# Block sums of gate weights made in the weight queue, a second plain pair at the change of x, and other pacing in a two-sequence encoder layer

## The chip, the cores and the metric

The kernel runs on one core of a Trainium2 chip. The metric is the device time of one execution in microseconds (us); less is better. The engines are TensorE (PE, with its weight loads shown as PEld), VectorE (DVE), ScalarE (ACT), GpSimd (POOL) and SyncE (SP), which issues the transfers that matter here.

## The reference

One encoder layer is applied to two sequences, a prompt of 1024 tokens and a sample of 2048 tokens, each with 16 learned meta tokens ahead of it. All arrays are float32.

```python
def _encoder_layer(h, ...):
    xn = _rmsnorm(h, g_pre)
    proj = xn @ w_in + b_in                      # 1024 -> 6672 columns
    na_q, na_k, na_v, na_z, ml_qk, ml_v, ml_z, ml_o, ml_g, mg = jnp.split(proj, SPLIT_IDX, axis=-1)
    ya = _neighbourhood_attention(na_q, na_k, na_v, na_rpb)     # 8 heads of 64
    ya = (ya * jax.nn.silu(na_z)) @ w_a
    yb = (_mlstm_branch(ml_qk, ml_v, ml_g, ml_o, conv_w, head_g) * jax.nn.silu(ml_z)) @ w_b
    ga, gb = jnp.split(jax.nn.sigmoid(mg), 2, axis=-1)          # 2 x 1024 gate columns
    y = (ga * ya + gb * yb) @ w_out
    return h + _rmsnorm(y, g_post)
```

The neighbourhood attention looks at windows of 8 rows by 16 columns in a grid 64 wide, and at the meta tokens. The mLSTM runs in both directions in chunks of 64 tokens.

## The kernel before

**Arithmetic.** Every float32 factor is split into a high and a low half (`xh`, `xl`; `whi`, `wlo`), and each product is three matmuls, high by high, low by high and high by low (`mm3`, L185 to L187).

**Order.** The order of TensorE's instructions is written out by hand; a scheduler places the instructions of the other engines and the transfers, all of which but a few are issued on SP's queue, and that queue is in order. Two generators give the order. `dense()` walks `PLAN`: groups of columns of the input projection for a sequence s and a half t0 of it, then six final blocks of 512 tokens (merge, output projection, norm).

```python
PLAN = ((0, 0, "m"), (0, 0, "n"), (1, 0, "m"), (1, 1024, "m"), (1, 1024, "n"), (1, 0, "n"), (1, 0, "g"), (1, 1024, "g"), (0, 0, "g"), ("f", 0, 0), ...)
```

"m" are the mLSTM's columns, "n" the attention's, "g" the 16 blocks of gate columns; s = 0 is the prompt, s = 1 the sample. `sparse()` gives the steps of the recurrence and of the attention: `ml` of s = 0, `na` of s = 0, `ml` of s = 1, `na` of s = 1. `run()` puts the two together: each step of the sparse generator yields a credit (`A_NA` for the attention, `A_A` and others for the mLSTM), and the dense generator then runs until the costs of its matmuls (`C512` = 0.235 for one of 512 columns) have used the credit up. A greater credit thus puts more dense matmuls beside each step.

**Weights.** A queue (`requests`) lists all weights in the order of their use. `wload` (L249) fetches the raw ones into one of two buffers (`wraw`, L257); `wpump` (L260) splits them on ACT (L286) and DVE (L287) into one of four pairs of buffers (`whi`, `wlo`; `NBW` = 4), and stores the halves for later uses (L307); a weight that was kept comes back by two loads (L279). `wtake` takes the next ones of the queue and `wdone` gives a buffer back and pumps on. The 16 weights of the merge and the output projection (kinds "m" and "o") are split and stored ahead of time, one ahead of each job of the groups 3 to 5 of `PLAN` (7, 5 and 4 of them). A job is four columns in feature-major form, or one token-major unit (`tm_unit`).

**Gates of the sample.** For s = 1 the gate columns are worked out in pairs of column blocks by a Strassen-Winograd scheme with seven products in place of eight (`sgates`): 84 matmuls of 512 columns for a pair, half and group where the plain way has 96. It needs sums of blocks of the weights and of x. The sums of weights are made by `wprep`: for each of the eight pairs two raw loads of 512 KB (`pr`), sums on DVE (`ps`), a split on ACT (`po`, L560) and on DVE (L561), and eight stores (`q..<-po`, L564). `wprep` is a side generator that is advanced at every second turn (`pace`) of the dense generator (`beside`); its first loads go out in the opening, and its transfers reach into (0,0,n). The sums of x are made by `tprep` (L588 to L599, stores at L602), at (1,1024,n) and (1,0,n), also as a side generator. At the gates the sums are loaded back (`whi<-q`, L272; `t1h` and so on, L855).

**The change of x.** Between (1,0,g) and (1,1024,g) the sample's other half must be loaded (`xload`, L863, and the sums of x, L855). `lead(j)` names the pairs that are worked out plainly at the start of such a group, as they need only x itself; there is one, pair 0. Each plain pair is run on the first 512 tokens and then on the second.

**Places that the prediction speaks of.** L1206 loads the mLSTM's gates (`g_t`). L1062 to L1089 are the attention's loads for one head pair (`gt`, `qr`, `kr`, `vr`, `zt`), L637 and L645 the stores of projected columns (`mq`, `nq`, `nz`), L527 the stores of split x for later groups, L1126 to L1173 the attention's scores, transposes and outputs.

Of the kernel before, what the change touches and what calls it, by code (L numbers as in the profile page):

```python
# [9 lines left out]
F32 = mybir.dt.float32  # L10
F32R = mybir.dt.float32r
I32 = mybir.dt.int32
AF = mybir.ActivationFunctionType
ALU = mybir.AluOpType
# [3 lines left out]
P = 128  # L18
TCARGS = dict(schedule_with_timeline_sim=True)
D = 1024  # L20
KT = D // P
# [9 lines left out]
C_MQ, C_MK, C_MV, C_MZ, C_MO, C_GA, C_GB = 2048, 2560, 3072, 3584, 4096, 4624, 5648  # L31
# [9 lines left out]
PLAN = ((0, 0, "m"), (0, 0, "n"), (1, 0, "m"), (1, 1024, "m"), (1, 1024, "n"), (1, 0, "n"), (1, 0, "g"), (1, 1024, "g"), (0, 0, "g"), ("f", 0, 0), ("f", 0, 1), ("f", 1, 0), ("f", 1, 1), ("f", 1, 2), ("f", 1, 3))  # L41
SW = ((1, 0), (1, 1024))
OPS = ("11", "12", "21", "22", "s1", "s2", "s3", "s4")
STEPS = (("ml", 0, ()), ("na", 0, (0, 1)), ("ml", 1, ()), ("na", 1, (0, 1, 2, 3)))
KC0 = (0, 8, 24, 40)
NKB = (3, 4, 4, 3)
# [83 lines left out]

NBW = 4
C512, C256 = 0.235, 0.12
A_NA, A_D, A_A, A_G = 1.085, 1.63, 1.82, 1.3


class K:
# [3 lines left out]
    def __init__(self, tc, ins, outs):  # L140
        self.tc, self.nc = tc, tc.nc
        self.xs = []
        self.i, self.o = ins, outs
        self.wreq, self.wraw, self.wrdy, self.wout = deque(), deque(), deque(), 0
        self.wseen, self.wkept, self.xkept = set(), {}, {}
        self.rwait = {}
        self.xput, self.turn, self.last, self.turns = deque(), 0, None, False
        self.need = False
        self.hold, self.early = deque(), True
        self.side, self.qd, self.TD = None, {}, {}  # L150


    def rsqrt8(self, pool, v, shape):
# [94 lines left out]

    def wload(self, most=2):  # L249

        while self.wreq and sum(x[1] is not None for x in self.wraw) < most:
            key, src, nk, w = self.wreq.popleft()
            raw = None
            if key[0] != "q" and key not in self.wseen:
                self.wseen.add(key)
                raw = self.wrp[0].tile([P, 4 * WU], F32, name="wraw", bufs=self.wrp[1])
                self.nc.sync.dma_start(raw[:, :nk * w], src)  # L257
            self.wraw.append((key, raw, nk, w))

    def wpump(self, most=NBW, parts=1, copy=None):  # L260


        nc, wp = self.nc, self.wp
        self.wload()
        while self.wraw and self.wout < most:
            key, raw, nk, w = self.wraw.popleft()
            n = nk * w
            hi = wp.tile([P, 4 * WU], F32R, name="whi", bufs=NBW)
            lo = wp.tile([P, 4 * WU], F32R, name="wlo", bufs=NBW)
            if key[0] == "q":  # L270
                for x, k in zip((hi, lo), key[1:]):
                    nc.sync.dma_start(x[:, :n].bitcast(F32), self.qd[k][:, :])  # L272
                self.wrdy.append([x[:, :n].rearrange("p (h k c) -> p h k c", h=2, k=4) for x in (hi, lo)])
                self.wout += 1
                self.wload()
                continue
            if raw is None:
                for x, d in zip((hi, lo), self.wkept[key]):
                    nc.sync.dma_start(x[:, :n].bitcast(F32), d[:, :])  # L279
            else:  # L280
                for a in range(parts):
                    c = slice(a * n // parts, (a + 1) * n // parts)
                    if copy:
                        copy(hi[:, c], raw[:, c])
                    else:
                        nc.scalar.activation(hi[:, c], raw[:, c], AF.Copy)  # L286
                    nc.vector.tensor_tensor(lo[:, c], raw[:, c], hi[:, c].bitcast(F32), op=ALU.subtract)  # L287
                self.wkept[key] = []
                for x, part in ((hi, "h"), (lo, "l")):
                    d = self.dp.tile([P, n], F32, name=f"w{part}{len(self.wkept)}")  # L290
                    self.hold.append((d, x[:, :n].bitcast(F32)))
                    self.wkept[key].append(d)
                if not self.early:
                    self.wflush()
                if key[0] in "mo":
                    self.wrdy.append(None)
                    self.wout += 1
                    self.wload()
                    continue
            self.wrdy.append([x[:, :n].rearrange("p (k c) -> p k c", k=nk) for x in (hi, lo)])  # L300
            self.wout += 1
            self.wload()
# [5 lines left out]

    def wtake(self, n):
        self.wpump()  # L310
        while self.wrdy[0] is None:
            self.wrdy.popleft()
            self.wdone()
        return [self.wrdy.popleft() for _ in range(n)]

    def wdone(self, n=1):
        self.wout -= n
# [125 lines left out]
    def build_half(self, s, t0, res):  # L443

        nc, wp = self.nc, self.wp
        if (s, t0) in self.xkept:
            yield
            yield "scaled"
            x = []
# [7 lines left out]
        if s == 0:  # L457
# [22 lines left out]
            def rows():  # L480
                self.rrows(dg, self.rr[:, 1], "sm")
                self.RD = self.dp.tile([P, D], F32, name="rrd")
                nc.sync.dma_start(self.RD[:, :], self.rr.rearrange("p a t -> p (a t)"))
                self.xp.close()
                self.side, self.pace = self.wprep(), 2
            self.rwait[s, t0] = rows
        else:
            bp = self.bp
# [47 lines left out]
    def wprep(self):  # L536
# [3 lines left out]
        with self.tc.tile_pool(name="pq", bufs=1, side="right", reuse_waits="tile") as pool:  # L540
            raws = {}

            def load(p):
                if p < 8:
                    raws[p] = pool.tile([P, 2, 2, 512], F32, name="pr", bufs=2)
                    for f in range(2):
                        nc.sync.dma_start(raws[p][:, f].rearrange("p a c -> p (a c)"), self.i["wu"][unit["i", C_GA + (2 * p + f) * P, P], :, :D])

            load(0)
            load(1)  # L550
            for _ in range(4):
                yield
            for p in range(8):
                raw = raws.pop(p)
                sm = pool.tile([P, 4, 512], F32, name="ps", bufs=1)
                todo = [((p, "11"), (p, "12"), raw[:, 0]), ((p, "21"), (p, "22"), raw[:, 1]),
# [219 lines left out]

    def lead(self, j):

        return [] if PLAN[j - 1][:2] == PLAN[j][:2] else [0]

    def requests(self):

        unit = {k: j for j, k in enumerate(_weight_units())}
        ahead = deque([("m", f, P) for f in range(KT)] + [("o", c, a) for c in range(4) for a in range(2)])
        for j, (s, t0, cols) in enumerate(PLAN):
            if s == "f":
                assert not ahead
                keys = [("m", f, P) for f in range(KT)] + [("o", c, a) for c in range(4) for a in range(2)]
            else:
                keys = []  # L790
                for kind, c in self.layout(cols):
                    if j >= 3 and ahead:
                        keys.append(ahead.popleft())
                    if cols == "g":
                        continue
                    keys += [("i", x, P) for x in c] if kind == "fm" else [("t", *c, a) for a in range(2)]
                if cols == "g":
                    assert not ahead
                    pairs = list(range(8))
                    lead = pairs if (s, t0) not in SW else self.lead(j)  # L800
                    keys = [("q", (p, f + "1"), (p, f + "2")) for p in lead for f in "12"]
                    pairs = [p for p in pairs if p not in lead]
                    if pairs:
                        seq = _sw_order(pairs)
                        keys += [("q", *seq[x:x + 2]) for x in range(0, len(seq), 2)]
            for k in keys:
                if k[0] == "q":
                    self.wreq.append((k, None, KT, P))
                    continue
                nk, w = (KT, P) if k[0] in "im" else (4, k[2] if k[0] == "t" else 256)  # L810
                self.wreq.append((k, self.i["wu"][unit[k], :, :nk * w], nk, w))
# [16 lines left out]

    def gopen(self):

        assert not any(x[1] is not None for x in self.wraw)
        self.left.close()
        self.gp, self.bp = self.left.enter_context(self.tc.tile_pool(name="gp", bufs=1, reuse_waits="tile")), None

# [100 lines left out]
    def group(self, s, t0, meta, cols, reuse, nxt):  # L935
# [3 lines left out]
        nb = None  # L939
        sw = (s, t0) in SW and cols == "n"  # L940
        if sw:
            self.side, self.pace = self.tprep(s, t0), 2
            sw = (s, t0, "g") in PLAN[:PLAN.index((s, t0, "n")) + 2]
        for j, (kind, c) in enumerate(jobs):
            if kind == "tm":
# [49 lines left out]
    def na(self, s, rts):  # L995
# [3 lines left out]
        with tc.tile_pool(name=f"na{s}{rts[0]}", bufs=1, side="right", reuse_waits="tile") as np_:  # L999
# [12 lines left out]
            for k in range(6):  # L1012
                next(prep, None)
                for _ in range(2 if k else 17 - 11 * s):
                    yield A_NA
            cur, nxt = self.head, None
            units = [(j, cb) for j in range(n) for cb in range(4)]
            ready = {}
# [1 line left out]
            for u in range(n_ + 4):  # L1020
                if u >= 4:
                    self.na_copy(ready[u - 4])
                if u < n_:
# [6 lines left out]
                    self.na_scores(np_, ready[u], rows)  # L1030
                    if j + 1 < n and cb == 0:
                        self.na_bias(rows, heads, j + 1)
                yield A_NA
                if u < n_:
                    self.na_exp(np_, ready[u])
                if 1 <= u <= n_:
# [4 lines left out]
                    next(prep, None)  # L1041
                if u == n_ + 3:
                    break
                yield A_NA
                if 2 <= u <= n_ + 1:
                    self.na_turn(np_, ready[u - 2])
                    if u < n_ and cb >= 2:
                        next(prep, None)
                yield A_NA
                if 2 <= u <= n_ + 1:  # L1050
                    self.na_low(ready[u - 2])
                if u >= 3:
                    self.na_out(ready[u - 3])
                yield A_NA

    def na_bias(self, rows, heads, j):

# [1003 lines left out]
```

## Time and profile before

| | before |
|---|---|
| median of 3 runs | 2819.14 us (2814.47 to 2819.79) |
| profiled execution | 2815.92 us |
| its span | 2814.2 us |
| its mean granted TensorE clock | 0.982 |
| HBM | 516.46 MB read, 244.69 MB written |

The stages of the plan start, in the profiled execution and by the order of TensorE's instructions, at 7.7 us (0,0,m), 277.7 (0,0,n), 508.0 (1,0,m), 774.2 (1,1024,m), 1063.3 (1,1024,n), 1278.5 (1,0,n), 1503.7 (1,0,g), 1690.1 (1,1024,g), 1901.9 (0,0,g), and the last final block at 2690.3. `na` of s = 0 begins at 779.8, `ml` of s = 1 at 1181.3 and `na` of s = 1 at 1998.0. Times in the profile are us from the start of the span, means of one instruction are in ns. The bracket behind an instruction of the time line is the idle time of its engine ahead of it, and what ended it.

### The profile page before, as it was taken

Reading aid. Unit: us, or ns where it says so; the run is one execution under the profiler, and the core shown is the slowest. Engines: PE = TensorE matmul, PEld = TensorE weight load, DVE = VectorE, ACT = ScalarE, POOL = GpSimd, SP = SyncE. Lnnn points to the kernel's source line nnn. Section 1 sums busy time; section 2 is a strip of 40 time slices with the busy share of each in tenths; the row PEclk is TensorE's granted clock in tenths of the full one; section 3 lists DMA queues with packets and bytes.
Section 4 is the critical chain, followed back from the end, with each engine's and each line's share of the span. In section 5 each row is a group of like instructions: output and inputs, shape, how many; then the busy total and the mean of one; then the engine's idle time right before and its main releaser. Section 6 shows DMA issues by size and latency. Waiting matters only on the chain.

```text
span 2814.2 us, 47371 instructions
## 1 busy us (share of the span) xinstructions
PE 2703.1 (96%) x16132; PEld 2379.4 (85%) x16132; DVE 1887.8 (67%) x5176; ACT 1394.3 (50%) x3305; POOL 16.3 (1%) x100
## 2 busy tenths in 40 slices
PE   9699799999999999999999997999999999999988
PEld 7599698889878988887798885888888998989978
DVE  4445478866657665467866754757468889798864
ACT  5332355653446455355546553555355655655531
POOL 0000000000000000000000000000000000000000
PEclk9899899999999999999999998999999999999989
DMA  9999666966697756479778889888669798998945
GB/s 364 397 387 365 238 211 229 365 204 199 213 352 267 228 194 214 158 246 341 269 251 283 278 284 351 289 284 296 190 195 303 242 323 271 298 323 265 322 163 212
DMA packets 397970, 764.32 MB, mean 272 GB/s; under 512 B 50240, under 2 KB 179216, under 8 KB 396192
## 3 DMA queue, kind: packets, MB, share of 16 engines
q1 hardware_dynamic: 396608, 758.61, 79.6%
q0 software_dynamic: 1120, 2.69, 0.4%
q8 instruction: 127, 2.08, 0.3%
q14 instruction: 115, 0.94, 0.1%
HBM read 516.46 MB, written 244.69 MB: 270 GB/s over the span
## 4 chain that ended last, share of the span: by engine, by line
PE 84%; DMA 10%; DVE 3%; ACT 1%; SPq 1%; issue 1%; DVEq 0%; POOL 0%; ACTq 0%; POOLq 0%
PE pj L185 12%; PE pj L187 12%; PE pj L186 12%; PE pj L707 5%; PE pj L708 5%; PE pj L709 5%; PE pj L890 3%; PE pj L892 3%; PE pj L891 3%; PE pj L1824 3%; PE pj L1826 3%; PE pj L1825 3%; PE sm L1173 3%; PE tr L1158 2%; DMA xl<-xl 1%; DMA xt<-xt 1%
## 5 line engine op out<-in xcount | busy, mean ns | idle before, releaser
L185 PE MATMUL pj<-xh,whi 128*128 128x512 f32 (+1 forms) x1360 | 535.7, 394 | 46.2 <-ACT st L627 23.1
L186 PE MATMUL pj<-xl,whi 128*128 128x512 f32 (+1 forms) x1360 | 523.0, 385 | 5.5 <-DMA xl<-xl 5.1
L187 PE MATMUL pj<-xh,wlo 128*128 128x512 f32 (+1 forms) x1360 | 521.8, 384 | 3.7 <-DMA wlo<-wl 3.4
L185 PEld LDWEIGHTS pj<-xh,whi 128*128 128x128 f32 x1360 | 258.5, 190 | 92.0 <-ACT st L627 23.5
L707 PE MATMUL pj<-whi,xh 128*128 128x256 f32 (+1 forms) x1152 | 329.0, 286 | 0.6 <-DVE stT L722 0.6
L708 PE MATMUL pj<-wlo,xh 128*128 128x256 f32 (+1 forms) x1152 | 324.9, 282 | 0.0
L709 PE MATMUL pj<-whi,xl 128*128 128x256 f32 (+1 forms) x1152 | 324.7, 282 | 0.0
L187 PEld LDWEIGHTS pj<-xh,wlo 128*128 128x128 f32 x1360 | 258.2, 190 | 58.1 <-DMA wlo<-wl 4.7
L186 PEld LDWEIGHTS pj<-xl,whi 128*128 128x128 f32 x1360 | 258.7, 190 | 47.7 <-DMA xl<-xl 5.6
L1824 PE MATMUL pj<-whi,mh 128*128 128x256 f32 x768 | 220.6, 287 | 0.7 <-DMA whi<-wh 0.7
L707 PEld LDWEIGHTS pj<-whi,xh 128*128 128x128 f32 x1152 | 216.9, 188 | 1.0 <-DVE stT L722 0.8
L708 PEld LDWEIGHTS pj<-wlo,xh 128*128 128x128 f32 x1152 | 217.0, 188 | 0.1
L709 PEld LDWEIGHTS pj<-whi,xl 128*128 128x128 f32 x1152 | 217.0, 188 | 0.0
L1826 PE MATMUL pj<-whi,mlo 128*128 128x256 f32 x768 | 216.3, 282 | 0.0
L1825 PE MATMUL pj<-wlo,mh 128*128 128x256 f32 x768 | 216.0, 281 | 0.0
L185 PE MATMUL pj<-yh,whi 128*128 128x512 f32 x384 | 155.0, 404 | 5.1 <-ACT yh L1742 5.1
L1165 DVE TENSOR_TENSOR pts<-tr,pts 96x384 fp32r<-96x384 f32 (+2 forms) x192 | 118.8, 619 | 57.2 <-ACT pts L1160 55.3
L187 PE MATMUL pj<-yh,wlo 128*128 128x512 f32 x384 | 152.3, 397 | 0.0
L186 PE MATMUL pj<-yl,whi 128*128 128x512 f32 x384 | 152.0, 396 | 0.0
L1160 ACT ACTIVATE pts<-tr 96x384 fp32r<-96x384 f32 (+2 forms) x192 | 103.5, 539 | 89.8 <-PE tr L1158 89.2
L1824 PEld LDWEIGHTS pj<-whi,mh 128*128 128x128 f32 x768 | 145.1, 189 | 1.8 <-DMA whi<-wh 0.9
L1825 PEld LDWEIGHTS pj<-wlo,mh 128*128 128x128 f32 x768 | 145.1, 189 | 0.9
(367 smaller groups left out, 6142.9 us busy)
## 6 DMA issues: line engine op xcount, KB each, us to landing
whi<-wh SPq DMA_DIRECT2D x160, 512.0 KB
wlo<-wl SPq DMA_DIRECT2D x160, 512.0 KB
wraw<-wu SPq DMA_DIRECT2D x48, 512.0 KB
wh<-whi SPq DMA_DIRECT2D x48, 512.0 KB
wl<-wlo SPq DMA_DIRECT2D x48, 512.0 KB
gt<-st SPq DMA_DIRECT2D x96, 256.0 KB
tg<-gt SPq DMA_DIRECT2D x96, 256.0 KB
whi<-q SPq DMA_DIRECT2D x43, 512.0 KB
```

Source lines behind the costliest of these rows:

```text
L185: mm(out, ah, bh, start=start, stop=False)
L186: mm(out, ah, bl, start=False, stop=False)
L187: mm(out, al, bh, start=False, stop=stop)
L707: nc.tensor.matmul(o, xh, wh, start=k == 0, stop=False)
L708: nc.tensor.matmul(o, xh, wl, start=False, stop=False)
L709: nc.tensor.matmul(o, xl, wh, start=False, stop=k == KT - 1)
L890: mm(bank, w[:, 0, k], xh[:, k], start=fresh and k == 0, stop=False, skip_group_check=True)
L1160: nc.scalar.activation(pts[:ks, :nb, 0, :], pt[:ks, :nb], AF.Copy)
L1165: self.nc.vector.tensor_tensor(pts[:ks, :nb, 1, :], pt[:ks, :nb], pts[:ks, :nb, 0, :].bitcast(F32), op=ALU.subtract)
L1824: nc.tensor.matmul(o, mh[:, k, xs], wh, start=clear > 0 and k == 0, stop=False)
L1825: nc.tensor.matmul(o, mh[:, k, xs], wl, start=False, stop=False)
L1826: nc.tensor.matmul(o, ml[:, k, xs], wh, start=False, stop=clear < 2 and k == KT - 1)
```

## The change

There are three parts.

1. **Block sums.** `wprep` makes the sums of the first three pairs only (`EARLY`), at every fourth turn in place of every second, and after six idle turns in place of four. For the other five pairs there are 20 entries ("p", pair, n) in the weight queue, four for each pair. Entries 0 and 1 fetch the two raw blocks, which stay in the two raw buffers (`pk`) until entry 3 is through; entries 2 and 3 make the sums in place on DVE. Each entry is split, in halves of 512 columns, into a `whi` and a `wlo` buffer, and stored by two transfers of 512 KB. `AHEAD` spreads these entries and then the 16 merge and output weights over groups 2 to 5 of the plan: 7, 7, 6 entries of sums in groups 2, 3 and 4, 6 merge weights in group 4 and 10 in group 5. They now stand between the weights of a job, where before the merge weights stood ahead of a job.
2. **Two plain pairs.** `lead` gives pairs 0 and 1 at the change of x.
3. **Pacing.** The attention's credit is 0.94 for s = 0 (1.085 before) and stays 1.085 for s = 1; `A_A` is 1.79 (1.82 before); `tprep` is advanced at every third turn (second before).

The counts of the built kernels: 16120 matmuls on TensorE (16108 before), 3004 activations (2987), 2455 two-tensor operations on DVE (2437), 2400 transfers on SP (2403).

```diff
+EARLY = 3
+AHEAD = ((0, 0), (0, 0), (1, 1), (1, 1), (2, 3), (2, 4))
-A_NA, A_D, A_A, A_G = 1.085, 1.63, 1.82, 1.3
+A_N, A_D, A_A, A_G = (0.94, 1.085), 1.63, 1.79, 1.3
...
     def wload(self, most=2):
-        while self.wreq and sum(x[1] is not None for x in self.wraw) < most:
-            key, src, nk, w = self.wreq.popleft()
+        while self.wreq:
+            key, src, nk, w = self.wreq[0]
             raw = None
-            if key[0] != "q" and key not in self.wseen:
+            if src is not None and key not in self.wseen:
+                if sum(x[1] is not None for x in self.wraw) + len(self.pk) >= most:
+                    break
...
+    def wsums(self, key, raw, x):
+        nc = self.nc
+        _, p, n = key
+        if raw is not None:
+            self.pk.append(raw[:, :D].rearrange("p (a c) -> p a c", a=2))
+        r = self.pk
+        sub = lambda o, a, b: nc.vector.tensor_tensor(o, a, b, op=ALU.subtract)
+        if n == 2:
+            nc.vector.tensor_tensor(r[1][:, 1], r[1][:, 0], r[1][:, 1], op=ALU.add)
+            sub(r[1][:, 0], r[0][:, 0], r[1][:, 0])
+        elif n == 3:
+            sub(r[0][:, 0], r[1][:, 1], r[0][:, 0])
+            sub(r[0][:, 1], r[0][:, 1], r[0][:, 0])
+        v = r[n % 2 if n < 2 else 3 - n]
+        for q, op in enumerate((("11", "12"), ("21", "22"), ("s3", "s1"), ("s2", "s4"))[n]):
+            h = x[q][:, :512]
+            nc.scalar.activation(h, v[:, q], AF.Copy)
+            nc.vector.tensor_tensor(x[q][:, 512:D], v[:, q], h.bitcast(F32), op=ALU.subtract)
+            d = self.qd[p, op] = self.dp.tile([P, D], F32, name=f"q{p}{op}")
+            nc.sync.dma_start(d[:, :], x[q][:, :D].bitcast(F32))
+        if n == 3:
+            self.pk = []
...
     def wpump(self, most=NBW, parts=1, copy=None):
+            if key[0] == "p":
+                self.wsums(key, raw, (hi, lo))
+                self.wrdy.append(None)
+                self.wout += 1
+                self.wload()
+                continue
...
     def wtake(self, n):
         self.wpump()
-        while self.wrdy[0] is None:
-            self.wrdy.popleft()
-            self.wdone()
-        return [self.wrdy.popleft() for _ in range(n)]
+        out = []
+        while len(out) < n:
+            x = self.wrdy.popleft()
+            if x is None:
+                self.wdone()
+            else:
+                out.append(x)
+        return out
...
-                self.side, self.pace = self.wprep(), 2
+                self.side, self.pace = self.wprep(), 4
...
-        return [] if PLAN[j - 1][:2] == PLAN[j][:2] else [0]
+        return [] if PLAN[j - 1][:2] == PLAN[j][:2] else [0, 1]
...
     def requests(self):
-        ahead = deque([("m", f, P) for f in range(KT)] + [("o", c, a) for c in range(4) for a in range(2)])
+        merge = [("m", f, P) for f in range(KT)] + [("o", c, a) for c in range(4) for a in range(2)]
+        ahead = deque([("p", p, n) for p in range(EARLY, 8) for n in range(4)] + merge)
...
-                for kind, c in self.layout(cols):
-                    if j >= 3 and ahead:
-                        keys.append(ahead.popleft())
+                for n, (kind, c) in enumerate(jobs):
+                    mine = [("i", x, P) for x in c] if kind == "fm" else [("t", *c, a) for a in range(2)]
+                    more = AHEAD[j][kind == "tm"] if j < 5 or n + 1 < len(jobs) else 0
+                    for u, k in enumerate(mine):
+                        for _ in range((u + 1) * more // len(mine) - u * more // len(mine)):
+                            if ahead:
+                                keys.append(ahead.popleft())
+                        keys.append(k)
...
-            self.side, self.pace = self.tprep(s, t0), 2
+            self.side, self.pace = self.tprep(s, t0), 3
...
-                yield A_NA
+                yield A_N[s]
```

More of the change, by code (lines that the diff above doesn't have):

```diff
@@ L257, in wload @@
                 self.nc.sync.dma_start(raw[:, :nk * w], src)
+            self.wreq.popleft()
             self.wraw.append((key, raw, nk, w))
+    def wsums(self, key, raw, x):
[19 more added lines that the diff above has]
+        if n == 3:
+            self.pk = []
     def wpump(self, most=NBW, parts=1, copy=None):
@@ L543, in load @@
             def load(p):
-                if p < 8:
+                if p < EARLY:
                     raws[p] = pool.tile([P, 2, 2, 512], F32, name="pr", bufs=2)
@@ L550, in wprep @@
             load(1)
-            for _ in range(4):
+            for _ in range(6):
                 yield
-            for p in range(8):
+            for p in range(EARLY):
                 raw = raws.pop(p)
@@ L787, in requests @@
                 assert not ahead
-                keys = [("m", f, P) for f in range(KT)] + [("o", c, a) for c in range(4) for a in range(2)]
+                keys = merge
+            elif cols == "g":
+                assert not ahead
+                pairs = list(range(8))
+                lead = pairs if (s, t0) not in SW else self.lead(j)
+                keys = [("q", (p, f + "1"), (p, f + "2")) for p in lead for f in "12"]
+                pairs = [p for p in pairs if p not in lead]
+                if pairs:
+                    seq = _sw_order(pairs)
+                    keys += [("q", *seq[x:x + 2]) for x in range(0, len(seq), 2)]
@@ L789, in requests @@
             else:
                 keys = []
-                for kind, c in self.layout(cols):
-                    if j >= 3 and ahead:
-                        keys.append(ahead.popleft())
[L794 to L805, printed above, removed]
+                jobs = self.layout(cols)
@@ L806, in requests @@
             for k in keys:
-                if k[0] == "q":
+                if k[0] == "q" or k[0] == "p" and k[2] > 1:
                     self.wreq.append((k, None, KT, P))
+                    continue
+                if k[0] == "p":
+                    self.wreq.append((k, self.i["wu"][unit["i", C_GA + (2 * k[1] + k[2]) * P, P], :, :D], KT, P))
                     continue
@@ L829, in gopen @@
     def gopen(self):
-        assert not any(x[1] is not None for x in self.wraw)
+        assert not self.pk and not any(x[1] is not None for x in self.wraw)
         self.left.close()
@@ L1032, in na @@
                         self.na_bias(rows, heads, j + 1)
-                yield A_NA
+                yield A_N[s]
                 if u < n_:
@@ L1043, in na @@
                     break
-                yield A_NA
+                yield A_N[s]
                 if 2 <= u <= n_ + 1:
@@ L1048, in na @@
                         next(prep, None)
-                yield A_NA
+                yield A_N[s]
                 if 2 <= u <= n_ + 1:
@@ L1053, in na @@
                     self.na_out(ready[u - 3])
-                yield A_NA
+                yield A_N[s]
     def na_bias(self, rows, heads, j):
```

## The prediction

> **What bounds the kernel now.** I read the page's totals first, then TensorE's waits, then the time line and the chain around each long wait, and last the order in which the instructions of both built kernels stand on each queue.
>
> ```profile
> span 2814.2 us, 47371 instructions
> PE 2703.1 (96%) x16132; PEld 2379.4 (85%) x16132; DVE 1887.8 (67%) x5176; ACT 1394.3 (50%) x3305; POOL 16.3 (1%) x100
> PE pj L185 <- ACT st L627: 23.1, 1, 23.1
> ```
>
> TensorE is busy for 2703.1 of 2814.2 us. The change leaves its work nearly alone, so all that it can win lies in the 111.1 us of idle time (2814.2 - 2703.1), and what it can lose are new holes. The largest hole, 23.1 us (third row: idle total, times, longest), lies in the opening, where both kernels issue the same transfers in the same order; it stays. The other large holes are three, and the change touches each. The run profiled took 2815.92 us, 1.7 us more than its span; the median of the three runs is 2819.14, 3.2 us above it. I make the sum against 2815.92.
>
> **The block sums leave the opening.** In the time line (start, duration, engine, line, tiles; in brackets the idle time before and its releaser), the chain and the windows (PE, PEld, DVE, ACT, POOL busy, PEclk, DMA share, GB/s):
>
> ```profile
> 296.69 3.27 SPq L564 DMA_DIRECT2D q7s<-po  x4
> 304.33 0.42 SPq L1206 DMA_DIRECT2D g_t<-gg  x1
> 298.86 5.02 DMA q7s<-po
> 310.86 1.07 PE L1233 MATMUL sm<-g_lf,tri 128*128 128x36 f32 x4 [16.06 <-DVE g_lf L1227]
> 311.00:317.00 6.00, 6.00 (x23) 4.47 (x23) 1.51 (x6) 0.49 (x3) 0.00 (x0) 0.61 0.00 0
> ```
>
> The last sums of pair 7 are stored at 296.69, land 5.02 us after 298.86, and only then do the gates of the mLSTM (g_t) load, at 304.33; TensorE stands for 16.06 us. It then runs 6 us at a granted clock of 0.61, which loses (1 - 0.61) x 6 = 2.3 us. In the changed order the last store of the three early pairs stands ahead of this place, and g_t's load has moved far ahead of it: -18.3 us (bounds: 0 if the load still meets a wait, -18.3). What is late next here is nothing that the trace shows; the stage behind it has its weights.
>
> The Trainium skill, "TensorE: Matmul & The Clock Gate", Part 1, has the array drop to half speed after an idle window of about 3.4 us and come back after as long a busy one; the 0.61 after the 16.06 us hole agrees. By the page a hole over 3.4 us loses about 1.7 us of clock (an estimate) where I take 2.3, which would make the sum less than 1 us lower.
>
> The work itself goes into later stages:
>
> ```profile
> L560 ACT ACTIVATE po<-pr 128x1024 fp32r<-128x1024 f32 x16 | 16.8, 1050 | 5.8 <-DMA pr<-wu 3.4 <-DMA q<-po 2.0 <-DMA q0s<-po 0.4
> L561 DVE TENSOR_TENSOR po<-pr,po 128x1024 fp32r<-128x1024 f32 x16 | 19.5, 1220 | 8.3 <-ACT po L560 8.3
> 290.00 0.69 ACT L622 ACTIVATE st<-pj,bq 128x512 f32<-128x512 f32 x1 [3.02 <-DVE pj L620]
> ```
>
> Twenty entries of 1.05 us ACT and 1.22 us DVE, now in halves of 512. Two halves take 2 x 0.69 us (third row) where a whole takes 1.05, a third more: 7 us of ACT and at most 8 us of DVE over four stages. ACT (50%) and DVE (67%) hide that except where DVE is full, which I cost below. It costs nothing as work; it costs as order.
>
> **One more pair done plainly at the change of x.**
>
> ```profile
> 1720.11 0.80 PE L185 MATMUL pj<-xh,whi 128*128 128x512 f32 x1 [15.24 <-DMA xh<-xh]
> 1725.98 0.80 PE L186 MATMUL pj<-xl,whi 128*128 128x512 f32 x1 [5.08 <-DMA xl<-xl]
> 1690.00:1705.00 15.00, 14.86 (x79) 12.50 (x77) 9.89 (x35) 8.27 (x23) 0.00 (x0) 1.00 1.03 407
> 1705.00:1726.00 21.00, 0.82 (x2) 0.31 (x2) 4.72 (x23) 1.82 (x5) 0.00 (x0) 0.58 1.04 403
> 530.20 0.40 PE L185 MATMUL pj<-xh,whi 128*128 128x512 f32 x1
> 530.43 0.40 PE L186 MATMUL pj<-xl,whi 128*128 128x512 f32 x1
> ```
>
> The stage starts at 1690. TensorE has work for 15 us (48 plain matmuls on the first half of x, 31 others), then stands 20.3 us (15.24 + 5.08), as the second half of x arrives 36 us after the start. The DMA engines are full over the whole stretch (share 1.03 and 1.04). The changed kernel moves the same x and sums there, so I keep the 36 us. It has 96 plain matmuls at 0.233 us (spacing of the last two rows), 22.4 us, and some 5.2 us of the mLSTM between: 27.6 us of work, so 8.4 us of hole. That wins 11.9 us. A plain pair costs 96 matmuls per stage against 84: 12 x 0.233 = 2.8 us. Together -9.1 us (bounds: +2.8 if x is later by as much, -14.7 if it came in 30 us).
>
> **The pace: neighbourhood attention ends before the last block.**
>
> ```profile
> 2698.83 1.22 PE L1173 MATMUL sm<-pts,vt 104*128 104x256 f32 x4 [3.49 <-ACT prb L1141]
> 2703.10 0.60 PE L1126 MATMUL sm<-kd,stk 128*128 128x312 f32 x1 [1.07 <-ACT prb L1141]
> 2709.50 0.62 PE L1173 MATMUL sm<-pts,vt 104*128 104x256 f32 x3 [0.59 <-DVE pts L1165]
> 2717.29 0.79 PE L185 MATMUL pj<-yh,whi 128*128 128x512 f32 x1 [5.07 <-ACT yh L1742]
> 2690.00:2720.00 30.00, 19.63 (x87) 16.02 (x86) 17.88 (x61) 10.10 (x29) 0.00 (x0) 0.75 0.19 63
> ```
>
> Now it ends 66 instructions into the last final block; its last units and the block's y wait for each other (3.49 + 1.07 + 0.59 + 5.07 = 10.2 us), with the clock at 0.75 over the 30 us. In the changed order it ends 204 matmuls ahead of that block, so other matmuls fill these waits: -10.2, and 1.5 of clock, -11.7 us (bounds 0 and -11.7). The same density costs elsewhere: each unit of s = 0 has some 13% less dense work beside it (0.94 against 1.085). Its chain of scores, exponentials and transposes then shows in places, between 0 and the 5.2 us (3.49 + 1.07 + 0.59) that it shows at the end, where it has none beside it. I take +2. The slower pace of the x sums puts their vector work at the same place in the built order, so nothing.
>
> **The new places in the weight queue.** SP issues in order, so a load behind a store waits for what the store waits for. The Trainium skill, "DMA: Bandwidth & Descriptors", Anatomy of one DMA, says the same: the DMA engines wait on no semaphore, the issuing sequencer does, ahead of dispatch. That speaks against this change; g_t at 304.33, behind the sums' stores, agrees. The changed order puts the load of the fourth column's weights 0 to 12 TensorE instructions ahead of its use at several starts of stages, behind stores of the columns before, since its slot comes free later with sum tiles between. At (1,0,m):
>
> ```profile
> 524.88 0.42 SPq L637 DMA_DIRECT2D mq<-st  x1
> 525.39 3.68 SPq L527 DMA_DIRECT2D xh<-xh  x6
> 529.17 2.19 SPq L527 DMA_DIRECT2D xl<-xl  x2
> 500.00:550.00 50.00, 50.00 (x249) 41.63 (x249) 43.27 (x143) 36.05 (x88) 0.20 (x2) 1.00 1.00 355
> 2782.62 4.61 DMA whi<-wh
> 1689.14 11.75 DMA whi<-q
> ```
>
> The load now stands behind these stores of mq and x, so it goes out at 529.1 to 531.4; the column is wanted at 530.7, when the third one's last matmuls (530.20, 530.43) are through. A weight needs 4.61 to 11.75 us to land (the last two rows, start and duration), with the DMA engines full here (share 1.00) nearer the middle: 8 us of hole and 2.3 of clock, +10.3 (bounds 0 and +14). At (1,1024,m):
>
> ```profile
> 774.40 0.47 PE L185 MATMUL pj<-xh,whi 128*128 128x512 f32 x1 [1.80 <-DMA whi<-wh]
> 785.92 0.50 PE L187 MATMUL pj<-xh,wlo 128*128 128x512 f32 x1 [2.48 <-DMA wlo<-wl]
> 791.35 0.42 SPq L1062 DMA_DIRECT2D gt<-rpb  x1
> 794.59 0.72 SPq L1089 DMA_DIRECT2D zt<-nz  x1
> 798.17 1.47 SPq L527 DMA_DIRECT2D xh<-xh  x2
> 798.66 0.39 PE L186 MATMUL pj<-xl,whi 128*128 128x512 f32 x1
> ```
>
> The late load stands behind the attention's seven loads (791.35 to 795.3) and x's stores (to 799.6), and is wanted at 798.9. By the long landing it is there at 811.4: 12.5 of hole and 2.3 of clock; the two waits of now, 4.3 us, lie in front of it and go: +10.5 (bounds -4.3 and +17). One more such load stands ahead of the first token-major unit of (1,1024,n): +4, by the 4.61 (0 to +12). At (1,0,n):
>
> ```profile
> 1314.73 0.36 PE L1574 MATMUL sc<-q,kh 128*128 128x256 f32 x1 [3.75 <-DVE den L1624]
> 1344.68 0.36 PE L1574 MATMUL sc<-q,kh 128*128 128x256 f32 x1 [2.62 <-DVE den L1621]
> 1362.47 1.01 PE L1705 MATMUL tr<-ident,hb 128*128 128x128 f32 x4 [3.67 <-DVE hb L1700]
> 1300.00:1350.00 50.00, 43.64 (x212) 36.26 (x212) 47.37 (x121) 32.14 (x80) 0.10 (x1) 0.97 0.93 311
> 1304.18 0.32 SPq L602 DMA_DIRECT2D t0h<-xr  x1
> ```
>
> Here DVE is full (47.37 of 50) and TensorE waits for it three times, 10.0 us. The fourth load now stands behind the store of column three and those of the x sums (as at 1304.18), which wait for this full DVE: by the long landing 11.75 and 2.3 of clock, 14 us. Two more weights with no lead cost 4.61 each, 9 us. Six more merge weights are split here (10 against 4), 7.3 us of DVE, of which I let 5 show. That is 28 us in place of the 10.0: +18 (bounds -5 and +30).
>
> **Sum:** -18.3 - 9.1 - 11.7 = -39.1; +2 + 10.3 + 10.5 + 4 + 18 = +44.8; +5.7 us, 2815.92 + 5.7 = 2821.6, so 2822. A measurement of this kernel tells about 0.2% (5.6 us) from no change.
>
> **Rivals.** *The late loads are in time.* If the sequencer stands less long than the order allows, each of six late loads costs what a late weight costs now (2.48) less the 4.3 that go, 10.6; with +2 for attention and the DVE waits as they are, -39.1 + 12.6 = -26.5, so 2789. For it: the trace shows many loads land in 4.61. Against: at 304.33 a queue wait was paid in full. *The queue's waits add up (slower).* If all six late loads land like the 11.75 row behind full DMA engines, each costs some 4.2 us more than I took (mean of mine 7.6): +5.7 + 25 = +31, 2847. It decides once the DMA share of (1,0,m) and (1,1024,m) stays at 1.0 until the late load. For it: shares of 1.00 and 0.93 already. *x comes later.* With the extra weights ahead of it, the second half of x is needed and late alike: the 11.9 go, 2834. *The gates' wait is not removed*, as g_t meets another late store: +18.3, 2840.
>
> **How the numbers follow.** The forecast gets 0.43 (2810 to 2834: 12 either way, the distance from its largest cost, 18, to that one's upper bound), loads in time 0.30, queue adds up 0.15, x later 0.07, gates' wait stays 0.05. Faster by over 0.2%: all of loads in time and 0.04 of the forecast, 0.34. Within 0.2%: 0.18, from the forecast alone. Slower: the rest, 0.21 + 0.15 + 0.07 + 0.05 = 0.48. The range leaves out half of the worst case and a little of the best: 2792 to 2844.
>
> **What would show it.** Right: no hole near 295 to 311; about 8 us behind 96 plain matmuls at the second stage of gates; no wait at the last final block; holes of 8 to 14 us released by whi or wlo at the fourth columns of (1,0,m), (1,1024,m) and (1,0,n). Wrong: those fourth columns start with holes under 3 us (then 2789), or with over 15 us each (then 2847).

## The result and the profile after

| | before | after |
|---|---|---|
| median (10 runs each) | 2816.85 us (2811.64 to 2819.79) | 2825.02 us (2822.89 to 2828.5) |
| ratio, 95% interval | | 1.0031 [1.0021, 1.004] |
| profiled execution | 2815.92 us | 2825.11 us |
| its span, granted clock | 2814.2 us, 0.982 | 2823.4 us, 0.980 |

The change makes the kernel slower by 0.31%, some 8.7 us. The forecast was 2822. The page of the changed kernel begins:

```profile
span 2823.4 us, 47431 instructions
PE 2708.3 (96%) x16144; PEld 2383.2 (84%) x16144; DVE 1886.9 (67%) x5194; ACT 1394.2 (49%) x3322; POOL 16.2 (1%) x100
```

The span grew by 9.2 us. TensorE is busy for 5.2 us more, of which the 12 matmuls of the second plain pair are 2.8 (12 x 0.233); the granted clock is lower too (0.982 to 0.980). Its idle time grew from 111.1 to 115.1 us (2823.4 - 2708.3). This small difference hides a large exchange. TensorE's waits of the changed kernel (idle total, times, longest):

```profile
PE pj L188 <- DMA whi<-wh: 29.9, 4, 12.5
PE pj L188 <- ACT st L667: 23.9, 1, 23.9
PE pj L747 <- DMA whi<-wh: 18.6, 2, 13.3
PE pj L190 <- DMA wlo<-wl: 6.0, 3, 2.8
PE pj L188 <- DMA wlo<-q: 5.9, 2, 3.6
PE pj L748 <- DMA wlo<-wl: 4.9, 2, 3.8
```

But for the opening's 23.9 us, all the waits at the head of the list are now for weights or their sums; before, the longest waits for a loaded weight were 1.80 us (whi) and 2.48 us (wlo). The windows (PE, PEld, DVE, ACT, POOL busy, PEclk, DMA share, GB/s) show what went:

```profile
290.00:311.00 21.00, 20.64 (x99) 15.27 (x98) 7.57 (x39) 7.72 (x19) 0.00 (x0) 1.00 0.16 53
311.00:317.00 6.00, 6.00 (x28) 4.85 (x27) 3.78 (x10) 3.32 (x8) 0.00 (x0) 1.00 0.99 342
1740.00:1770.00 30.00, 23.86 (x95) 19.15 (x94) 10.05 (x39) 8.29 (x21) 0.00 (x0) 0.83 1.03 404
2690.00:2720.00 30.00, 30.00 (x254) 30.00 (x253) 10.17 (x22) 8.95 (x28) 0.00 (x0) 1.00 0.57 195
2720.00:2750.00 30.00, 30.00 (x151) 25.29 (x151) 18.34 (x40) 4.95 (x13) 0.00 (x0) 1.00 0.78 270
```

The gates' hole near 300 us is gone, and the clock behind it is 1.00; at the change of x (now at 1733) 6.1 us of idle are left in the window in place of 20.3; and the last attention units (2690 to 2720) and the start of the last block, which is now at 2724.6 with the attention done at 2697, have no idle time (last two rows). And this is what came, in the time line of TensorE and of SP, with two steps of the chain:

```profile
515.99 0.77 PE L188 MATMUL pj<-xh,whi 128*128 128x512 f32 x1 [4.42 <-DMA whi<-wh]
792.21 0.77 PE L188 MATMUL pj<-xh,whi 128*128 128x512 f32 x1 [12.50 <-DMA whi<-wh]
1186.89 0.58 PE L747 MATMUL pj<-whi,xh 128*128 128x256 f32 x1 [13.30 <-DMA whi<-wh]
1326.63 0.79 PE L188 MATMUL pj<-xh,whi 128*128 128x512 f32 x1 [10.63 <-DMA whi<-wh]
1392.49 0.79 PE L190 MATMUL pj<-xh,wlo 128*128 128x512 f32 x1 [2.77 <-DMA wlo<-wl]
1435.21 0.58 PE L747 MATMUL pj<-whi,xh 128*128 128x256 f32 x1 [5.26 <-DMA whi<-wh]
...
779.36 0.69 SPq L1109 DMA_DIRECT2D gt<-rpb  x1
783.77 0.35 SPq L1136 DMA_DIRECT2D zt<-nz  x1
784.50 0.34 SPq L315 DMA_DIRECT2D whi<-wh  x1
784.50 7.58 DMA whi<-wh
...
1179.40 0.48 SPq L315 DMA_DIRECT2D whi<-wh  x1
1318.55 0.42 SPq L642 DMA_DIRECT2D t1h<-xr  x1
1321.06 0.63 SPq L315 DMA_DIRECT2D whi<-wh  x1
```

At (1,1024,m) the fourth column is wanted at 779.7 (792.21 - 12.50). Its load goes out at 784.50, behind the attention's loads, and takes 7.58 us to land. At 1173.6 (1186.89 - 13.30) and 1316.0 (1326.63 - 10.63) the loads are late too: they go out 5.8 and 5.1 us after they are wanted, the second behind stores of the x sums.

### The profile page after: what moved, and what is told of

The parts are those of the page before. It is cut to its first block, busy times and chain, and to the rows that moved or that the text cites. A ratio compares the mean times of both kernels' runs of the same rounds, so it can differ in the third digit from the quotient of the medians.

```text
span 2823.4 us, 47431 instructions
## 1 busy us (share of the span) xinstructions
PE 2708.3 (96%) x16144; PEld 2383.2 (84%) x16144; DVE 1886.9 (67%) x5194; ACT 1394.2 (49%) x3322; POOL 16.2 (1%) x100
## 2 busy tenths in 40 slices
DMA packets 397540, 762.76 MB, mean 270 GB/s; under 512 B 50193, under 2 KB 179169, under 8 KB 395761
## 3 DMA queue, kind: packets, MB, share of 16 engines
HBM read 514.89 MB, written 244.69 MB: 269 GB/s over the span
## 4 chain that ended last, share of the span: by engine, by line
PE 82%; DMA 10%; DVE 3%; ACT 2%; SPq 1%; issue 1%; DVEq 0%; ACTq 0%
PE pj L188 12%; PE pj L190 12%; PE pj L189 12%; PE pj L747 5%; PE pj L748 5%; PE pj L749 5%; PE pj L1871 3%; PE pj L1872 3%; PE pj L1873 3%; PE pj L937 3%; PE pj L939 3%; PE pj L938 3%; PE sm L1220 3%; PE tr L1205 2%; DMA wlo<-wl 1%
## 5 line engine op out<-in xcount | busy, mean ns | idle before, releaser
L188 PE MATMUL pj<-xh,whi 128*128 128x512 f32 (+1 forms) x1376 | 544.4, 396 | 57.5 <-DMA whi<-wh 29.9
L190 PE MATMUL pj<-xh,wlo 128*128 128x512 f32 (+1 forms) x1376 | 529.9, 385 | 6.3 <-DMA wlo<-wl 6.0
L189 PE MATMUL pj<-xl,whi 128*128 128x512 f32 (+1 forms) x1376 | 530.0, 385 | 0.1
```

The lines of the kernel that those rows point to most:

```text
L188: mm(out, ah, bh, start=start, stop=False)
L189: mm(out, ah, bl, start=False, stop=False)
L190: mm(out, al, bh, start=False, stop=stop)
```

## The experiments

Ratios are to the kernel before, measured beside it on the same chip; their medians before were 2814.0 to 2817.8 us.

| kernel | median, us | ratio, 95% interval |
|---|---|---|
| e1: change, entries ahead of a job | 2793.76 | 0.9927 [0.9915, 0.994] |
| e2: before, two plain pairs | 2796.23 | 0.9938 [0.9926, 0.9951] |
| e3: before, pacing | 2791.8 | 0.9918 [0.9904, 0.9931] |
| e4: before, two plain pairs and pacing | 2779.34 | 0.9871 [0.9856, 0.9886] |
| e5: before, slower sums of x | 2814.41 | 1.0002 [0.9994, 1.0011] |
| e6: before, attention credit of s = 0 | 2791.19 | 0.9916 [0.99, 0.9932] |
| e7: change, six pairs early, entries ahead | 2770.81 | 0.9848 [0.9834, 0.9861] |
| e8: before, block sums in the queue | 2831.51 | 1.0064 [1.0046, 1.0081] |
| e9: change, all entries ahead of jobs | 2809.34 | 0.997 [0.996, 0.9979] |
| e10: e7 with seven pairs early | 2783.28 | 0.9876 [0.986, 0.9891] |

**e1: the same work, other places in the queue.**

```diff
                     for u, k in enumerate(mine):
-                        for _ in range((u + 1) * more // len(mine) - u * more // len(mine)):
+                        for _ in range(0 if u else more):
```

> The changed kernel with one edit: the entries of sums and merge weights stand ahead of the first weight of a job, as the merge weights did in the kernel before, and not between its weights. Same work, same counts. Theory (place in the queue): the late loads are the fourth weights whose buffer is freed by an entry that stands just ahead of them. In the built order the leads of these loads at (1,0,m), (1,1024,m) and (1,0,n) grow from 0 to 12 TensorE instructions to 25 to 44; only the token-major units behind three or four merge weights keep 1 to 15. So the holes of 6.2, 12.5, 12.0 and 5.1 us at the fm jobs shrink to 2.5 us or less each (about -30 us with the clock), those at the token-major units (14.3 and 9.1) stay: 2795 us, ratio to before 0.99. Rival (volume: the added splits, stores and loads fill DMA, ACT and DVE in these stages): holes move but keep their sum, 2820 to 2828 us.

2793.76 us: the same entries in the same groups, moved by up to three places, take 1.0% of the changed kernel's time away (0.9927 against 1.0031). TensorE's time line keeps waits for a weight at the token-major units, and one of 2.4 us at a start of a stage:

```profile
761.66 0.47 PE L188 MATMUL pj<-xh,whi 128*128 128x512 f32 x1 [2.39 <-DMA whi<-wh]
1172.13 0.55 PE L747 MATMUL pj<-whi,xh 128*128 128x256 f32 x1 [6.52 <-DMA whi<-wh]
1402.81 0.58 PE L747 MATMUL pj<-whi,xh 128*128 128x256 f32 x1 [5.15 <-DMA whi<-wh]
```

The holes of 12.50 and 10.63 us are gone. The work is the same, so place, not volume, made these. Of the two waits that were expected to stay, the one of 14.3 us at (1,1024,n) fell to 6.52, and the one of 9.1 us at (1,0,n) is 10.5 with its waits for wlo (5.15 + 3.04 + 2.33).

**e2, e3 and e4: the other two parts without the first.**

```diff
-        return [] if PLAN[j - 1][:2] == PLAN[j][:2] else [0]
+        return [] if PLAN[j - 1][:2] == PLAN[j][:2] else [0, 1]      # e2, e4
...
-A_NA, A_D, A_A, A_G = 1.085, 1.63, 1.82, 1.3
+A_N, A_D, A_A, A_G = (0.94, 1.085), 1.63, 1.79, 1.3                 # e3, e4
-            self.side, self.pace = self.tprep(s, t0), 2
+            self.side, self.pace = self.tprep(s, t0), 3              # e3, e4
```

> The kernel before with two plain pairs at the change of x and nothing else. Theory: the 20.3 us hole near 1705 becomes 6 to 8 us and 12 more matmuls cost 2.8 us: -9 to -11.5, 2806 to 2808 us. Rival (x is only fetched later, as the extra weights stand ahead of it): the hole stays within 3 us of 20.3 and the time is +0 to +3 us.

> The kernel before with the pacing alone (0.94 for the attention of s = 0, 1.79, every third turn for the sums of x). Theory: the waits of 10.2 us and the slow clock at 2690 to 2720 go (-11.7), the denser attention costs up to 2: -10, 2807 us. Rival (the waits of the attention's tail only move to another place): -3 to +3 us.

> The kernel before with two plain pairs and the pacing, the block sums as before: the change without its first part. Theory: the two parts are at different places and add up, -20 us, 2797 us; the first part of the change then costs 28 us on top of it. Rival (they share a limit): -12 us or less, 2805 us.

All three came out better than expected: about 17, 23 and 36 us (the ratios' differences from 1 times the medians before). The parts nearly add up (17 + 23 = 40). Time line and window of e2 at the change of x, then the window from 2680 to 2720 of the kernel before, of e2 and of e3, and two stretches of the kernel before within it:

```profile
1718.56 0.50 PE L185 MATMUL pj<-xh,wlo 128*128 128x512 f32 x1 [3.08 <-DMA wlo<-q]
1727.01 0.61 PE L186 MATMUL pj<-xl,whi 128*128 128x512 f32 x1 [1.65 <-DMA xl<-xl]
1700.00:1740.00 40.00, 34.05 (x163) 27.58 (x162) 23.81 (x86) 18.12 (x52) 0.20 (x2) 0.96 0.98 367
...
2680.00:2720.00 40.00, 29.63 (x170) 26.01 (x170) 26.44 (x82) 16.61 (x45) 0.00 (x0) 0.81 0.23 82
2680.00:2720.00 40.00, 32.66 (x147) 26.32 (x146) 24.56 (x68) 11.29 (x30) 0.00 (x0) 0.87 0.46 158
2680.00:2720.00 40.00, 40.00 (x207) 34.02 (x207) 22.50 (x47) 5.58 (x14) 0.00 (x0) 1.00 0.78 278
...
2698.20:2708.40 10.20, 8.34 (x34) 7.41 (x35) 7.92 (x28) 4.60 (x14) 0.00 (x0) 0.50 0.00 1
2715.30:2722.10 6.80, 4.81 (x11) 3.50 (x12) 2.76 (x4) 1.26 (x2) 0.00 (x0) 0.50 0.39 115
```

In e2 the plain matmuls cover x but for 1.65 us, and 5.95 us of the 40 are idle, where the kernel before has 20.32 (15.24 + 5.08). Less the 2.8 us of the 12 matmuls that is 11.6 us. The rest of e2's 17 us lies elsewhere: from 2680 to 2720 its idle time is 7.3 us in place of 10.4, at a clock of 0.87 in place of 0.81. So the second part alone already takes some of the waits of the attention's tail, which the pacing takes whole: in e3 these 40 us have no idle time and a clock of 1.00. That both parts draw on these waits fits their sum being 4 us short; no run shows it by itself.

**e5 and e6: which of the pacing's edits.** e5 has the third turn for the sums of x alone, e6 the 0.94 alone.

> The kernel before with the sums of x advanced at every third turn instead of every second, and nothing else. The pacing of e3 took 22 us off where the prediction's steps gave 10; it also removed two of the three waits for DVE near 1310 to 1362 us. Theory as predicted (the sums' vector work stays at the same place in the order): 2811 to 2818 us, no change, the three waits stay. Rival (this pace is what removed those waits): -6 to -11 us, 2803 to 2809 us, with less than 5 us left of the 10.0.

> The kernel before with the attention credit of s = 0 at 0.94, and nothing else of the pacing. Theory (the earlier end of the attention of s = 0 moves all later recurrence and attention against the dense work): it takes most of e3's gain, -15 to -20 us, 2795 to 2800 us, with no wait of the attention's tail at the last final block, and the waits for DVE at (1,0,n) under 5 us. Rival (the mLSTM's credit 1.79 or the sums' pace took it): -8 us or less.

e5 is no change, e6 has all of e3's gain. In e5 the waits for DVE at (1,0,n) did not go but came together in one (first row); in e6 a shorter one is left (second row), and the page shows less busy time for the same matmuls:

```profile
1364.88 1.15 PE L1705 MATMUL tr<-ident,hb 128*128 128x128 f32 x4 [13.70 <-DVE hb L1700]
...
1325.60 0.58 PE L1574 MATMUL sc<-q,kh 128*128 128x256 f32 x1 [3.73 <-DVE q L1528]
PE 2695.5 (97%) x16132; PEld 2376.0 (85%) x16132; DVE 1886.0 (68%) x5176; ACT 1388.9 (50%) x3305; POOL 16.3 (1%) x100
span 2790.3 us, 47387 instructions
```

Of e6's 23.9 us of span, 16.3 are idle time (111.1 to 94.8) and 7.6 are busy time of TensorE (2703.1 to 2695.5) with the count unchanged. The slow clock is about half of these 7.6. Over all stretches with a granted clock of 0.5 in the traces, TensorE is busy for 43.9 us in the kernel before and for 36.7 in e6, and half of the difference, 3.6 us, is what the clock gives back; what the other 4.0 are is open. The largest piece lies in the tail, where the two stretches above lose 6.6 us, half of 8.34 + 4.81. The Trainium skill, "TensorE: Matmul & The Clock Gate", Part 1, describes it, half speed after an idle window of about 3.4 us until a busy one has passed. The two stretches at 0.50 agree. In the kernel before, though, shorter holes of 1.80 and 2.48 us (774.40 and 785.92) were each followed by 3.4 us at half clock, and one of 2.62 us (1344.68) was not; here the measurement decides.

**e8: the first part alone.** The changed kernel with `lead` of one pair, 1.085, 1.82 and the second turn.

> The kernel before with the first part of the change alone: sums of five pairs in the weight queue, entries between the weights, one plain pair and the old pacing. Theory: the gates' 16 us and 2 us of clock go; late loads (leads 0 to 3 instructions) cost 8 us at (1,0,m), 13 at (1,1024,m), 13 at (1,0,n), and at its last units some 10; with the clock +25 us on before, 2840 us (2832 to 2850). Rival (the parts only clash with each other): 2800 us or less, as 18 us go and nothing comes.

2831.51 us, +18 us where +25 was expected. Its waits for the fourth columns:

```profile
787.18 0.77 PE L188 MATMUL pj<-xh,whi 128*128 128x512 f32 x1 [7.01 <-DMA whi<-wh]
1308.92 0.77 PE L188 MATMUL pj<-xh,whi 128*128 128x512 f32 x1 [13.84 <-DMA whi<-wh]
```

The same part costs 18 us on the kernel before and 45 us on e4 (1.0031 / 0.9871 = 1.0162, each measured beside its own runs of the kernel before). Most of the 27 us between shows in three places. At (1,1024,m) the wait is 12.50 us in place of 7.01: in e8 the attention's loads don't stand ahead of this load, in the changed kernel they do. At (1,1024,n) the changed kernel has the 13.30 us at 1186.89, and e8 has a shorter wait there, 5.50 us for the gates at 1189.48. At (1,0,n) e8's late loads stand in place of the three waits for DVE of the kernel before, 10.0 us, which are gone; in e4 the pacing has already brought these down to 4.2 us (2.59 + 1.64), so there is less to be had. That it is the pacing which moves the attention's loads ahead of the late one is read from the order on the queue; no run has the first part with the pacing alone or with the second plain pair alone.

**e7, e9 and e10: how many entries, and where.** All three put entries ahead of a job, as e1.

```diff
-AHEAD = ((0, 0), (0, 0), (1, 1), (1, 1), (2, 3), (2, 4))
+EARLY, AHEAD = 6, ((0, 0), (0, 0), (1, 1), (1, 1), (2, 1), (1, 1))   # e7; wprep at turn 2, 4 idle turns
+EARLY, AHEAD = 3, ((0, 0), (0, 0), (2, 1), (2, 1), (3, 1), (3, 1))   # e9
+EARLY, AHEAD = 7, ((0, 0), (0, 0), (1, 1), (1, 1), (1, 1), (1, 1))   # e10; else as e7
```

> The changed kernel with six pairs made early at every second turn after four idle turns, the entries of the other two pairs and of the merge weights ahead of a job, at most two ahead of a feature-major job and one ahead of a token-major unit. In the built order no weight before the last block then has a lead under 30 TensorE instructions, and g_t loads 86 instructions ahead of its use. Theory (a late load costs, and the gates' wait goes when the sums' stores stand ahead of it): e4's 2779 less 18 us, 2761 us (2755 to 2768). Rival (the sums in later stages cost by their volume): over 2772 us.

> The changed kernel with all its 20 entries of sums kept in the queue, but ahead of jobs: two or three ahead of a feature-major job, one ahead of a token-major unit. It differs from e1 only in that the three and four merge weights ahead of token-major units are spread over more jobs. Theory (place): the holes of e1 at the token-major units (1165 to 1178 and 1397 to 1412 us, 20.3 us with no clock counted) go; leads of 2 to 30 TensorE instructions at the starts of three stages cost 2 to 5 us each: 2775 to 2785 us. Rival (volume: e7 beat e1 because it moves 12 entries fewer into the later stages): 2790 us or more, like e1's 2794.

> e7 with seven pairs made early in place of six. In the built order the sums' last stores still stand ahead of g_t, but only just, and g_t's load has no lead on its use (86 instructions in e7, and behind the sums' last stores in the kernel before). Theory (the gates' wait is the landing of g_t behind these stores): a hole of 5 to 12 us comes back near 290 us, 2777 to 2784 us. Rival (the wait goes with the transfers' volume in the opening, 10 MB of 40 or 5 of 40 fewer): under 3 us of hole and e7's 2771 within 4 us.

e7 is the fastest of all, 1.5% under the kernel before. It has no hole near 300 us (window) and one wait of over 1 us for a weight of the projections, where the kernel before had two. It missed its 2761 by 10 us. Against e4, a wait for DVE of 3.51 us is new, and another has grown from 2.59 to 6.51 (last two rows); what the rest is, the runs don't show:

```profile
285.00:311.00 26.00, 25.64 (x120) 19.34 (x119) 9.63 (x42) 9.17 (x23) 0.00 (x0) 1.00 0.19 68
766.29 0.47 PE L188 MATMUL pj<-xh,whi 128*128 128x512 f32 x1 [2.48 <-DMA whi<-wh]
478.88 0.55 PE L1621 MATMUL sc<-q,kh 128*128 128x256 f32 x1 [3.51 <-DVE q L1575]
1348.19 1.15 PE L1752 MATMUL tr<-ident,hb 128*128 128x128 f32 x4 [6.51 <-DVE hb L1747]
```

e9 refuted its own expectation. The waits at the token-major units went, as expected, but others came at the starts of stages (TensorE and SP):

```profile
787.25 0.77 PE L188 MATMUL pj<-xh,whi 128*128 128x512 f32 x1 [12.26 <-DMA whi<-wh]
772.92 0.65 SPq L286 DMA_DIRECT2D q5s<-whi  x1
779.72 0.32 SPq L315 DMA_DIRECT2D whi<-wh  x1
```

With two entries ahead of the job, half of the four buffers are taken; the first column's load goes out at 779.72, 6.8 us behind the store of an entry and 4.7 us after it is wanted (787.25 - 12.26 = 775.0). So to stand ahead of a job isn't enough: what counts here is the lead of a load on its use, and with four buffers each entry near a start takes lead from the columns. The change, e9 and e1 do the same work at ratios of 1.0031, 0.997 and 0.9927, so the place alone is worth 1% of the time. e7 also has 12 entries fewer in the queue, and no run tells what of its gain is their number and what their place. e10 shows the other end, the gates' wait:

```profile
300.13 1.07 PE L1280 MATMUL sm<-g_lf,tri 128*128 128x36 f32 x4 [4.99 <-DVE g_lf L1274]
```

With eight pairs early the hole is 16.06 us, with seven 4.99, with six none: the load of g_t goes out at 304.33, 289.99 and 268.96, and TensorE wants it near 295 (310.86 - 16.06, 300.13 - 4.99). Two pairs moved were enough; the change moved five.

## Why the prediction was right, and where it was right by accident

The direction and the size of the total came out (+5.7 forecast, +8.7 measured), but by luck: each part alone came out better than forecast, and together they cost more than alone, by nearly the same amount.

- **The gates' wait (-18.3).** As predicted: 16.06 us of hole gone, clock 1.00 behind it, and e7 and e10 show that it goes with the pairs made early. In e10 g_t's load stands 15.5 us behind the start of the last stores of sums (274.48), with other stores between, so it may be held by all that stands ahead of it on the queue and not by these stores alone, as the prediction has it; no run tells the two apart.
- **The change of x (-9.1).** The 8.4 us of hole forecast are 6.1, for weights of sums and not for x: 96 plain matmuls cover x nearly. In e2 the change of x gives 11.6 us. That the part is worth 17 alone is the tail of the attention, which the prediction gave to the pacing only.
- **The pace (-11.7 and +2).** Mis-sized: 23 us (e3, e6). The tail's 10.2 us of waits went as forecast. Its slow clock was put at 1.5 us and is 6.6, and the shift also shortens the waits for DVE at (1,0,n), from 10.0 to 3.9 us in e3 (2.27 + 1.65), which the prediction did not see. That the sums' pace does nothing held (e5).
- **The late loads (+10.3, +10.5, +4, +18).** The named places were right: holes of 4.42 + 1.80 us at (1,0,m) for the 8 forecast, 12.50 for 12.5 at (1,1024,m), 10.63 + 1.42 for 11.75 at (1,0,n), and 14.2 at its later weights for 9. The term of the token-major unit of (1,1024,n) was mis-sized: 14.3 (13.30 + 1.02) for 4, as I gave the load a lead of nothing and it went out 5.8 us late (1179.40 against 1173.6). This is the largest miss among the holes.
- **The sum.** Parts two and three were forecast at -18.8 (-9.1 - 11.7 + 2) and are -36 (e4). The first part was forecast at +24.5 and is +18 alone (e8). Alone, the parts are thus 24 us better than forecast (17 + 6.5). But on top of e4 the first part costs 45, so together the parts cost 27 us more than alone, and the sum put this at nothing. The reason lies in making it from one profile of the kernel before: the 10.0 us for DVE were counted as a saving of the late loads, while the pacing shortens the same waits, and the late loads were priced by the times of before. The total is near only because 24 and 27 have opposite signs.
- **Smaller slips.** The first step, that all that can be won is idle time, leaves out the busy time at half clock (43.9 us before). The lower bound at the change of x is -15.1 and not -14.7 (x in 30 us against 27.6 of work leaves 2.4 of hole). With 1.7 us of clock for 2.3 in all four places where the sum has it, the sum is 1.2 us lower, not less than 1.
- **The rivals.** "Loads in time" fell at 779.7, 1173.6 and 1316.0. "The queue's waits add up" was met in size by one of six late loads, that of (1,1024,n) with 14.3 us, but 5.8 of these are its late issue and not its landing. No wait for x was left in the changed kernel, and the gates' wait did go.

## What to carry to other kernels

A preparation that is moved off a full stretch into a queue of weights costs, as these runs show it, by the lead that it takes from the loads behind it, more than by its work. With four buffers, read for every load how many instructions lie between its issue and its use, and move only as much as the old wait asks for (two pairs here, not five). Where several edits meet, measure each alone and the rest without it; a change that moves the time by 0.3% held a gain of 36 us and a loss of 45, and 27 of the 45 came only with the other parts. Count the slow clock behind each hole as part of the hole, from the busy time at that clock; a window's mean clock counts idle time too.

## What the runs showed of the hardware that was not expected

A half of a weight (512 KB) that lands in 4.61 us near the end of the kernel before, with a DMA share of 0.46 from 2780 to 2788, took 7.58 us at 784.50 in the changed kernel with a share of 1.04, so the price of a missing lead differs by stage. In the stretch from 1740 to 1770 the DMA engines moved 404 GB/s, and nearly all that this kernel's transfers move is read from HBM or written to it (762.76 MB moved, 514.89 read and 244.69 written). The Trainium skill, "DMA: Bandwidth & Descriptors", Specifications, gives some 358 GB/s as the limit of one core to HBM, as half of what two cores share. This one core went beyond it, and here the measurement decides.
